# Splitting the first group's load 1 + 15 rows instead of 4 + 12 in a row-sum kernel

## The chip, the cores and the metric

The kernel runs on one core of one Trainium2 chip. The metric is the time of one execution on the device in microseconds (us). The profiled span, which begins with the first instruction, is some 1.8 us shorter than the timed value of the same execution.

## The reference

```python
def setup_inputs():
    batch, seq, dim = 32, 512, 1024
    return {"x": np.random.randn(batch, seq, dim).astype(np.float32)}

def reference(x):
    return np.sum(x, axis=-1).astype(np.float32)
```

That is 16,384 rows of 1,024 numbers, 67.1 MB to be read, and 64 KB to be written. Each number is added once.

## The kernel before

The rows are cut into eight groups of 8.39 MB. In a group each of the 128 partitions gets 16 consecutive rows of 4 KB. The sync engine (SP) issues all loads, on one queue. VectorE sums the rows, and ScalarE (ACT) helps at the end.

```python
    BIG = 16
    x_g = x.flatten_outer_dims().rearrange("(g p j) d -> g p j d", p=P, j=BIG)
    last = J // BIG - 1          # 7
    FIRST = 4
    ...
        tc.tile_pool(name="in", bufs=3) as inpool,
    ...
        def rows(t, a, n, j, n_act, pairs=False):
            nv = n - n_act
            block = t[:, a * dim : (a + n) * dim].rearrange("p (n d) -> p n d", d=dim)
            load = nc.sync.dma_start(out=block, in_=rows_from(j, n))
            ...
                sums_of.append(vec(sums[:, j : j + nv], block[:, :nv, :]))
    ...
        for g in range(last):
            t = inpool.tile([P, BIG * dim + 4], fp32)
            if g == 0:
                rows(t, 0, FIRST, 0, 0)
                first = sums_of[-1]
                rows(t, FIRST, BIG - FIRST, FIRST, 0)
                continue
            load = rows(t, 0, BIG, g * BIG, BIG // 2 if g == last - 1 else 0)
            if g == 1:
                hold(load, first, "no descriptors of later loads while the first ones start")
    # ... group 7 in smaller and smaller loads (8, 5, 2 rows, then one row in two pieces), and the stores
```

Group 0 arrives in two loads, so VectorE can begin before all of it is there. The load of group 1 is held until the first reduce has ended. There are three input buffers, so the load of group 3 waits until VectorE has finished with group 0.

## Time and profile before

| | before |
|---|---|
| time, median | 161.9 us (161.78 to 162.58) |
| span | 160.2 us |
| queue of the loads, share of 16 DMA engines' time | 97.7% |
| VectorE busy | 75% |
| period of a middle group | 19.35 us for 8.39 MB = 433.5 GB/s |

First look for the resource that is never idle. These are lines of the profile page of the kernel before: VectorE (DVE) busy time, its share and its number of instructions; then the DMA queues with packets, megabytes and share.

```profile
span 160.2 us, 125 instructions
DVE 120.1 (75%) x22; ACT 17.3 (11%) x31; POOL 0.2 (0%) x4
q1 hardware_dynamic: 2016, 67.12, 97.7%
```

The queue q1 carries the loads and is full for nearly the whole span. VectorE has a quarter of the time to spare. The timeline of VectorE shows where it spends that quarter. Its columns are start, duration, the operation with its shapes, and in brackets the idle time before it and what ended it.

```profile
7.16 4.42 DVE L130 TENSOR_REDUCE sums<-t 128x4 f32<-128x4096 f32 x1 [7.16 <-DMA t<-in_x_dram]
21.68 12.95 DVE L130 TENSOR_REDUCE sums<-t 128x12 f32<-128x12288 f32 x1 [10.10 <-DMA t<-in_x_dram]
41.05 17.22 DVE L130 TENSOR_REDUCE sums<-t 128x16 f32<-128x16384 f32 x1 [6.42 <-DMA t<-in_x_dram]
60.40 17.22 DVE L130 TENSOR_REDUCE sums<-t 128x16 f32<-128x16384 f32 x1 [2.13 <-DMA t<-in_x_dram]
...
137.82 8.69 DVE L130 TENSOR_REDUCE sums<-t 128x8 f32<-128x8192 f32 x1 [2.15 <-DMA t<-in_x_dram]
```

Every wait is for a load. VectorE always catches up (17.22 us of work for 19.35 us of data) and then waits 2.13 us.

The trace has a record of every DMA packet (start, duration, size). A packet here is one partition's contiguous piece of one load, and each of the 16 DMA engines carries 8 packets of each load. Usual durations are 611 ns for 16 KB, 1815 for 48 KB and 2418 for 64 KB. With these and the smaller ones, an engine's packets of the whole input take 155.07 us. The first data packet starts 1.0 us after the first issue, and the last one ends at 157.44 us. So the stream loses only 1.4 us in all (157.44 - 1.00 - 155.07).

### The profile page before, as it was taken

What the parts mean: (1) busy time and instruction counts of PE and PEld (TensorE: products, weight loads), DVE (VectorE), ACT (ScalarE), POOL (GpSimd) and SP (SyncE); (2) the same over time, 40 slices, a digit from 0 to 9 for tenths busy, and PEclk for the clock granted to TensorE, in tenths of its full rate; (3) what the DMA queues carried; (4) which work ended last, traced back from release to release, by engine and by line L of the source; (5) the groups of instructions that cost most, each with busy time, mean ns of one, the idle gap of its engine ahead of it and who ended that gap; (6) DMA issues with size and microseconds to landing.
All of it is one profiled execution on the core that took longest, in us unless ns stands there. A gap on an engine that the chain in (4) does not pass through costs nothing.

```text
span 160.2 us, 125 instructions
## 1 busy us (share of the span) xinstructions
DVE 120.1 (75%) x22; ACT 17.3 (11%) x31; POOL 0.2 (0%) x4
## 2 busy tenths in 40 slices
DVE  0280059960799959999499994999949998597943
ACT  3000000000000000000000000000000000596952
POOL 0000000000000000000000000000000000000000
DMA  7999996996996996996996997998969969999994
GB/s 262 458 466 515 393 523 262 523 523 262 523 523 262 523 523 262 523 523 262 523 491 294 523 458 327 523 409 376 523 262 523 523 262 523 393 393 425 409 379 112
DMA packets 2928, 67.18 MB, mean 419 GB/s; under 512 B 1264, under 2 KB 1392, under 8 KB 1520
## 3 DMA queue, kind: packets, MB, share of 16 engines
q1 hardware_dynamic: 2016, 67.12, 97.7%
q10 hardware_dynamic: 912, 0.06, 0.4%
HBM read 67.11 MB, written 0.07 MB: 419 GB/s over the span
## 4 chain that ended last, share of the span: by engine, by line
DMA 73%; DVE 25%; SPq 1%; issue 0%; DVEq 0%
DMA t<-in_x_dram 73%; DVE sums L130 24%; SPq L169 1%; SPq L210 0%; DVE t L144 0%; DVEq L241 0%
## 5 line engine op out<-in xcount | busy, mean ns | idle before, releaser
L130 DVE TENSOR_REDUCE sums<-t 128x16 f32<-128x16384 f32 (+3 forms) x9 | 116.6, 12953 | 35.5 <-DMA t<-in_x_dram 35.5
L157 ACT ACTIVATE unread<-t 128x1024 f32<-128x1024 f32 x15 | 15.2, 1010 | 139.6 <-DMA t<-in_x_dram 139.6
L144 DVE CUSTOM_DVE_ANT_0 t<-t 128x512 f32<-128x512 f32 (+2 forms) x6 | 3.5, 603 | 2.7 <-DMA t<-in_x_dram 2.6
L157 ACT ACTIVATION_READ_ACCUMULATOR unread<-t 128x1 f32 x15 | 2.8, 186 | 0.0
L157 ACT ACT_TABLE_LOAD x1 | 1.3, 1283 | 0.8 <-PEq L230 0.8
L144 DVE DVE_READ_ACCUMULATOR2_ANT sums<- 128x1 f32 x5 | 0.4, 84 | 0.0
L230 POOL MEMSET const-bfloat16-1.0<- 128x1 bf16 x1 | 0.1, 102 | 0.0
L230 POOL MEMSET const-uint8-127<- 128x1 uint8 x1 | 0.1, 102 | 0.0
L230 POOL MEMSET const-float32-0.0<- 128x1 f32 x1 | 0.1, 99 | 0.2 <-issue 0.2
L230 POOL MEMSET const-float32-1.0<- 128x1 f32 x1 | 0.1, 99 | 0.0
L144 DVE DVE_READ_ACCUMULATOR2_ANT t<- 128x1 f32 x1 | 0.1, 82 | 0.0
L208 DVE MEMSET t<- 128x1 f32 x1 | 0.1, 59 | 0.0
## 6 DMA issues: line engine op xcount, KB each, us to landing
t<-in_x_dram SPq DMA_DIRECT2D x1, 6144.0 KB, 20.9
t<-in_x_dram SPq DMA_DIRECT2D x1, 4096.0 KB, 31.3
t<-in_x_dram SPq DMA_DIRECT2D x1, 2560.0 KB, 37.3
t<-in_x_dram SPq DMA_DIRECT2D x1, 2048.0 KB, 7.1
t<-in_x_dram SPq DMA_DIRECT2D x1, 1024.0 KB, 39.3
t<-in_x_dram SPq DMA_DIRECT2D x1, 280.0 KB, 39.5
t<-in_x_dram SPq DMA_DIRECT2D x1, 232.0 KB, 39.6
t<-in_x_dram SPq DMA_DIRECT2D x6, 40.8
```

Source lines behind the costliest of these rows:

```text
L130: return nc.vector.tensor_reduce(out=dst, in_=src, axis=mybir.AxisListType.X, op=mybir.AluOpType.add)
L144: return nc.vector.tensor_tensor_reduce(out=src[:, :n], in0=src[:, :n], in1=src[:, n:], scale=1.0, scalar=0.0, op0=mybir.AluOpType.add, op ...
L157: nc.scalar.activation(out=unread[:, :n], in_=src, func=mybir.ActivationFunctionType.Copy, accum_out=dst,)
L169: load = nc.sync.dma_start(out=block, in_=rows_from(j, n))
L208: nc.vector.memset(whole[:, width + 1 :], 0.0)
L230: nc = _bacc.Bacc("TRN2", target_bir_lowering=False, num_devices=1)
```

## The change

The intent is to let VectorE start earlier: the first load is a quarter of the size, and the second has the other 15 rows. By the hold, the load of group 1 is also issued earlier.

```diff
     last = J // BIG - 1
-    FIRST = 4
+    FIRST = 1
     pieces = (560, 464)
```

## The prediction

> What bounds the kernel now. The DMA stream. The page shows 67.18 MB in a 160.2 us span; one queue's packets fill 97.7% of 16 engines' time. In the timeline VectorE starts group 1 at 41.05, group 2 at 60.40, up to 137.82 us: 19.35 to 19.37 us per 8.39 MB group, 433.5 GB/s. That agrees with the fabric ceiling of 435 GB/s in the Trainium skill, "DMA: Bandwidth & Descriptors", section "Where 436 GB/s comes from". VectorE is busy 75% and waits about 2.1 us for each load. The packet records show data on all 16 engines from 1.0 to 1.8 us after the first issue to 157.4 us, with gaps of at most 0.17 us: only the stream's start, its packets, and the tail after 157.4 us set the time.
>
> What the change moves. The first group is still two loads of 128 packets each, 8 per engine, same bytes, same order. Packet sizes go from 16 KB + 48 KB to 4 KB + 60 KB. Packet times before: 611 ns for 16 KB, 1815 for 48 KB, 2418 for 64 KB, 309 for 8 KB, so about 37.7 ns per KB plus some 8 ns per packet. Estimates: 4 KB 159 ns, 60 KB 2268. The pair sums to 2.43 us both ways, so stream time is unchanged.
>
> Start. Each engine's first packet took 0.74 to 1.47 us instead of 0.61, about 0.5 us of cold start. I expect it once per engine again, not per packet. The first load should land at about 7.1 minus 3.6 us (1.57 MB at 433.5 GB/s): 3.5 us, estimate. The second load is issued at 0.78 us in both; data followed the first issue by 1.0 us, so its packets should be ready by about 1.9 us, before the first load's packets run out near 2.8 us. No gap.
>
> VectorE. The reduce of four rows took 4.42 us and of twelve 12.95; of one row I estimate 1.22, of fifteen 16.15 (1.067 us per row plus 0.15). That load lands at 21.7 us as before, so its reduce ends at about 37.8 instead of 34.6 us. Group 1's data comes at 41.05: slack shrinks from 6.4 to about 3.2 us. Group 3's load waits for that buffer and is issued at 37.9 instead of 34.7 us; groups 1 and 2 keep the queue full until 60 us, so 22 us of cover remain. So nothing reaches the critical path.
>
> Hold. Group 1's load waits for the first reduce's end: now near 4.8 us, not 11.6. At 11.6 to 12.5 us before, with two issues, no 48 KB packet took over 1.825 us: no visible cost. And 4.8 us is after the cold packets, which ended by 2.9 us.
>
> Predicted: 161.9 us, range 161.4 to 162.6. Chances: faster by over 2% 0.01, within 2% 0.96, slower by over 2% 0.03.
>
> What would show it: same group starts at 41.05, 60.40 ... (within 0.3 us); idle before the fifteen-row reduce about 17 us instead of 10.1; last data packet near 157.4 us; the reduce of fifteen at 16.1 us.
>
> What would make it wrong: small first packets that each pay the cold start, or a second load whose descriptors come late, opening a gap at 2 to 4 us (up to about 1 us); the earlier issue of groups 1 and 2 slowing the stream at 5 us; 60 KB packets slower per byte than 48 and 64 KB ones.

## The result and the profile after

The changed kernel took 162.24 us (median of 6 runs, 162.05 to 162.25), the kernel before 161.97 us (6 runs, 161.78 to 162.58). The ratio is 1.0006, with a 95% interval of 0.9987 to 1.0025. Ratios here are the mean time of one kernel's runs over that of the other's of the same rounds, so not quite the ratio of the medians quoted.

The same lines of the page, of the changed kernel:

```profile
span 160.5 us, 125 instructions
DVE 120.1 (75%) x22; ACT 17.3 (11%) x31; POOL 0.2 (0%) x4
q1 hardware_dynamic: 2016, 67.12, 97.5%
```

And the timeline of its VectorE:

```profile
3.87 1.22 DVE L130 TENSOR_REDUCE sums<-t 128x1 f32<-128x1024 f32 x1 [3.87 <-DMA t<-in_x_dram]
22.28 16.15 DVE L130 TENSOR_REDUCE sums<-t 128x15 f32<-128x15360 f32 x1 [17.19 <-DMA t<-in_x_dram]
41.63 17.22 DVE L130 TENSOR_REDUCE sums<-t 128x16 f32<-128x16384 f32 x1 [3.20 <-DMA t<-in_x_dram]
...
138.38 8.69 DVE L130 TENSOR_REDUCE sums<-t 128x8 f32<-128x8192 f32 x1 [2.12 <-DMA t<-in_x_dram]
```

VectorE does start 3.29 us earlier (3.87 instead of 7.16 us). It then waits 17.19 us for the second load instead of 10.10. The larger second reduce leaves 3.20 us of slack before group 1 instead of 6.42.

One thing was not predicted. Group 1 starts at 41.63 instead of 41.05 us, 0.58 us later, although the bytes and the number of packets are the same. The packet records place it. In the table below, "excess" is the sum of the packets' durations over their usual ones, divided by 16, so that it is time per DMA engine.

| packet records | before | changed |
|---|---|---|
| first load: usual packet; excess | 611 ns; 0.58 us | 159 ns; 0.60 us |
| second load: usual packet; excess | 1815 ns; 0.00 us | 2267 ns; 0.33 us |
| second load: the 16 engines end | 20.97 to 21.27 us | 21.32 to 21.92 us |
| excess of the 32 KB and 20 KB packets (group 7) | 0.44 us | 0.02 us |
| last data packet ends | 157.44 us | 157.53 us |

The cold start costs the same 0.6 us with small packets as with large ones. But the second load's packets lost 0.33 us per engine, all of it in packets that started between 3 and 13 us, and the engines ended further apart. The reduce waits for the last engine, hence the 0.58 us. By the end of the stream only 0.1 us of it was left, since in this pair of profiles the kernel before lost 0.42 us more in its last group. (The balance is not negative because each engine of the changed kernel also spent 0.2 us more without a packet, 0.32 instead of 0.12.)

### The profile page after: what moved, and what is told of

Read it like the earlier page. It is cut to its first block, busy times and chain, and to the rows that moved or that the text cites. A ratio compares the mean times of both kernels' runs of the same rounds, so it can differ in the third digit from the quotient of the medians.

```text
span 160.5 us, 125 instructions
## 1 busy us (share of the span) xinstructions
DVE 120.1 (75%) x22; ACT 17.3 (11%) x31; POOL 0.2 (0%) x4
## 4 chain that ended last, share of the span: by engine, by line
DMA 75%; DVE 22%; SPq 1%; issue 0%; DVEq 0%
DMA t<-in_x_dram 75%; DVE sums L130 22%; SPq L169 1%; SPq L210 0%; DVE t L144 0%; DVEq L241 0%
## 5 line engine op out<-in xcount | busy, mean ns | idle before, releaser
L130 DVE TENSOR_REDUCE sums<-t 128x16 f32<-128x16384 f32 (+4 forms) x9 | 116.6, 12953 | 35.9 <-DMA t<-in_x_dram 35.9
## 6 DMA issues: line engine op xcount, KB each, us to landing
t<-in_x_dram SPq DMA_DIRECT2D x1, 7680.0 KB, 21.5
```

What stands on the lines that cost most here:

```text
L130: return nc.vector.tensor_reduce(out=dst, in_=src, axis=mybir.AxisListType.X, op=mybir.AluOpType.add)
```

## The experiments

Three questions are open. Is the prediction's reason right, that there is an unused reserve of time between VectorE and the stream (main theory), or do a gain and a loss merely cancel? How large is the reserve, and what would use it up? And where do the 0.33 us come from: from issuing groups 1 and 2 at 5.1 us, while the second load is young (theory I), or from the packets themselves (theory P)? Twelve runs were made: two repeats and ten other kernels. All gave correct results. A stream or an engine is said to run dry when it has no packet left to carry.

### The changed kernel and the kernel before, once more

No edit.

> The changed kernel once more, as a control. Main theory (the input stream sets the time, and the change leaves its bytes and its number of packets alone): 162.0 to 162.4 us, ratio to before within 0.4%. In the first profile of the changed kernel the 128 packets of 60 KB took together 0.32 us per DMA engine more than 2.267 us each, all before 12.5 us, and group 1 started at 41.63 instead of 41.05 us. If that belongs to the change it is here again (0.2 to 0.4 us per engine, group 1 at 41.4 to 41.8); if it was chance it is not (under 0.1, group 1 at about 41.1).

Measured: 162.13 us (ratio 1.0006, interval 0.9986 to 1.0025). The excess of the 60 KB packets is 0.34 us, and group 1 starts at 41.58 us. It came again, so it belongs to the change.

> The kernel before once more, as a control. 161.7 to 162.2 us. If the missing excess in the second load is its property, its 48 KB packets again take under 0.05 us per engine over 1.815 us, and group 1 starts at 41.0 to 41.4. In its first profile the late loads (32 KB and 20 KB packets) took 0.44 us per engine over their usual time, which the changed kernel's did not: if that is a property of it, it is here again (over 0.3); if chance, under 0.15.

Measured: 161.83 us (ratio to itself 1.0001). The second load's excess is again 0.00 us, and group 1 starts at 41.23 us. The excess in the last group is 0.22 us, between the two numbers expected. So the loss there is not settled as a property of the kernel before; it varies. Last data packet: 157.24 us, against 157.49 in the repeated changed kernel. It was run at another time.

### The hold at its old time, with one row first

```diff
                 rows(t, 0, FIRST, 0, 0)
+                for _ in range(5):
+                    sums_of.append(vec(sums[:, 0:1], t[:, :dim].rearrange("p (n d) -> p n d", d=dim)))
                 first = sums_of[-1]
```

> One-row first load, but its reduce is done six times, so that the loads of groups 1 and 2 are issued at about 11.2 us as before, not at 5.1. Theory I (the slow 60 KB packets come from issuing two large loads while the second load starts): their excess falls under 0.05 us per engine and group 1 starts at about 41.1. Theory P (they come from the small first packets or the 60 KB form itself): the excess stays 0.2 to 0.4 us per engine and group 1 starts at about 41.6. Both: the time stays within 0.4% of before, 161.8 to 162.4.

Measured: 162.26 us (ratio 1.0014, 0.9994 to 1.0034). Groups 1 and 2 were issued at 11.13 and 11.51 us. The excess is 0.33 us all the same, and group 1 starts at 41.59. VectorE's lines of this run:

```profile
3.62 7.49 DVE L130 TENSOR_REDUCE sums<-t 128x1 f32<-128x1024 f32 x6 [3.62 <-DMA t<-in_x_dram]
22.24 16.15 DVE L130 TENSOR_REDUCE sums<-t 128x15 f32<-128x15360 f32 x1 [11.13 <-DMA t<-in_x_dram]
41.59 17.22 DVE L130 TENSOR_REDUCE sums<-t 128x16 f32<-128x16384 f32 x1 [3.20 <-DMA t<-in_x_dram]
```

Theory I falls: with the issues put back to their old time, group 1 is as late as in the changed kernel.

### No hold at all, with one row and with four

```diff
-            if g == 1:
-                hold(load, first, "no descriptors of later loads while the first ones start")
```

> One-row first load and no hold: groups 1 and 2 are issued right after the second load, at 1.2 to 2 us. Main theory: 162.0 to 162.6, the packets are the same. Theory I adds an excess of 0.3 us or more per engine in the first two loads. Rival (the hold matters, and the small time difference hides a gain by one cause and a loss by another): over 163 us.

Measured: 162.14 us (ratio 1.0006), groups 1 and 2 issued at 1.15 and 1.63 us, an excess of 0.24 us, group 1 at 41.46 us. The 60 KB packets are slow as before, no slower.

> The kernel before without its hold: groups 1 and 2 issued at 1.2 to 2 us instead of 11.6. Main theory: 161.8 to 162.5. Theory I: the 16 KB and 48 KB packets now take 0.2 to 0.5 us per engine more than their usual 0.611 and 1.815 us beyond the cold start (before: 0.58 us of cold start and nothing on the 48 KB packets), and group 1 starts at 41.3 to 41.7. Theory P: as before, group 1 at about 41.05.

Measured: 161.89 us (ratio 0.9998, 0.9972 to 1.0023). The 48 KB packets have an excess of 0.00 us. The cold start is 0.56 us, and the last data packet ends at 157.23 us. So the hold buys nothing measurable here, and the early issue disturbed nothing. In this run group 1 started at 41.32 us because the engines ended their second load 0.64 us apart, with no excess at all; that spread came from the cold start, where one engine's first packet began at 1.90 us.

### The split moved the other way

```diff
-    FIRST = 1
+    FIRST = 12
```

> The same split moved the other way: 12 rows first, 4 second, the hold kept. Here the issue of group 1 does reach the critical path by the account of the stream: the first load lands at about 16.7 us, its reduce ends at 29.6, group 1 is issued then and its data starts 1.0 us later, while the first two loads end at 21.3. A gap of about 9.3 us in the DMA stream at 21 to 31 us, all later groups 9.3 us later, time about 171.3 us (170.3 to 172.3). If the place of the split and of the hold never matters, 162.

Measured: 172.42 us (ratio 1.0653, 1.0637 to 1.0669), just outside the expected range. Here the hold waits for a reduce that ends at 29.9 us, long after the two loads have. The view of three stretches of this run, with columns busy time of VectorE, ScalarE and GpSimd, clock, DMA share and GB/s:

```profile
16.00:21.00 5.00, 4.06 (x1) 0.00 (x0) 0.00 (x0) 1.00 0.98 419
21.00:31.00 10.00, 10.00 (x2) 0.00 (x0) 0.00 (x0) 1.00 0.12 39
31.00:36.00 5.00, 3.22 (x1) 0.00 (x0) 0.00 (x0) 1.00 0.86 341
```

The stream is dry for 9.7 us per engine (0.12 of a DMA share in the middle line). The expected gap of 9.3 us left out the restart: data came from the first engine 0.95 us after the issue and from the last 1.88 us after it, and each engine's first packet then took 0.64 us more than usual. That is a second cold start, as long as the one at entry.

### More vector work in group 0

```diff
                 rows(t, FIRST, BIG - FIRST, FIRST, 0)
+                for _ in range(N):      # N = 1: done twice; N = 2: three times
+                    sums_of.append(vec(sums[:, FIRST:BIG], t[:, FIRST * dim : BIG * dim].rearrange("p (n d) -> p n d", d=dim)))
```

> The changed kernel with the 15-row reduce done twice: 16.15 us more of vector work, five times what the change added there. Account of the cover: it ends at 54.6 us, before group 3's buffer is needed at about 60.9, and VectorE regains 2.13 us in each later group, just in time for the last loads. Time unchanged, 162.0 to 162.6. If vector work in the first group is on the critical path: 178.

Measured: 162.16 us (ratio 1.0021, 1.0006 to 1.0036). The 16.15 us of added work moved the end by about as much as the unchanged one-row kernel's own difference. The view of the waits gives the total in us, their number and the longest. In the changed kernel the reduces of line 130 waited for their data as follows:

```profile
DVE sums L130 <- DMA t<-in_x_dram: 35.9, 9, 17.2
```

In this run they waited less; the second line has the waits for the last small loads:

```profile
DVE sums L130 <- DMA t<-in_x_dram: 21.0, 2, 17.5
DVE t L144 <- DMA t<-in_x_dram: 1.8, 2, 1.1
```

Apart from the two waits of group 0, only 1.8 us are left, before the last small loads. So nearly all of the later slack of VectorE was used, and none of the stream: group 3's load was issued at 54.55 us, still 5.3 us before the first engine would have run dry.

> The 15-row reduce three times: 32.3 us more of vector work. It ends at 70.7 us, group 3's load is issued then instead of at 38.5, after the stream has run dry at 60.9: a gap of about 10.8 us in the stream, and VectorE still behind at the end. Worked out step by step: 177 us (175.5 to 178.5). If all of the added work counted: 194; if none: 162.

Measured: 176.49 us (ratio 1.0905, 1.0886 to 1.0923). The next step of the same size costs 14.3 us. Group 3's load was issued at 71.05 us, while the stream ran dry at 60.0 to 60.8. The view of three stretches shows it:

```profile
50.00:60.00 10.00, 9.97 (x2) 0.00 (x0) 0.00 (x0) 1.00 0.97 419
60.00:73.00 13.00, 13.00 (x2) 0.00 (x0) 0.00 (x0) 1.00 0.22 76
73.00:83.00 10.00, 10.00 (x1) 0.00 (x0) 0.00 (x0) 1.00 0.98 426
```

In the second run the last data packet ends 12.9 us later than in the changed kernel, and the span grows by 14.4: the other 1.5 us are VectorE's, which still lags behind when the last data arrive. So vector work in group 0 meets two limits: an issue that comes too late for the stream, and VectorE's catching up before the last loads, which the first run had nearly reached. That work was free at 16.15 us and not at 32.3; where in between it begins to cost was not measured.

### Two buffers instead of three

```diff
-        tc.tile_pool(name="in", bufs=3) as inpool,
+        tc.tile_pool(name="in", bufs=2) as inpool,
```

> The changed kernel with two buffers instead of three: group 3's load is issued when group 1's reduce ends, at 58.9 us, about 2.0 us before the stream would run dry, and data follows an issue by 1.0 us. Account of the cover: 162.2 to 163.5 us, no gap or a few tenths per group. Rival (the third buffer is what hides the change): five gaps of 1 us or more, over 167 us.

Measured: 168.83 us (ratio 1.0433, 1.0388 to 1.0478). The account of the cover missed here, and the time is in the rival's range. VectorE's timeline in this run:

```profile
61.28 17.22 DVE L130 TENSOR_REDUCE sums<-t 128x16 f32<-128x16384 f32 x1 [2.14 <-DMA t<-in_x_dram]
82.44 17.22 DVE L130 TENSOR_REDUCE sums<-t 128x16 f32<-128x16384 f32 x1 [3.94 <-DMA t<-in_x_dram]
102.34 17.22 DVE L130 TENSOR_REDUCE sums<-t 128x16 f32<-128x16384 f32 x1 [2.68 <-DMA t<-in_x_dram]
123.97 17.22 DVE L130 TENSOR_REDUCE sums<-t 128x16 f32<-128x16384 f32 x1 [4.41 <-DMA t<-in_x_dram]
```

The period of 19.35 us has become 19.9 to 21.6 us. Group 3 was issued at 59.17 us. The earliest engine ran dry at 59.96, only 0.80 us later, and not at 60.82, when the last one did. In this run the records put together 4.2 us of added idle time per engine (4.55 instead of 0.33) and 2.8 us of added excess (3.96 instead of 1.13), which makes up the 6.9 us of longer span. The excess is mostly cold first packets again, 0.22 to 0.58 us on average in each of the five loads after group 2. The engines drift apart as well: they end group 3 over 1.9 us, and group 5 over 2.8 us, where group 2 ended over 0.9.

The next kernel is the one before, with two buffers, to see whether the narrower spread of four rows first saves it.

> The kernel before, with two buffers. With one row first, two buffers gave 168.8 us: the earliest engine ran dry at 59.96 us, 0.80 us after group 3's issue, and data needs 1.1 us from issue to an idle engine. With four rows first the engines end within 0.3 us of one another instead of 0.9, so the cover is 1.34 us (58.30 to 59.64). Theory (the spread between engines decides): no gap, 161.9 to 163. Rival (two buffers are too few in any case): about 167 to 170, as with one row.

Measured: 167.52 us (ratio 1.0348, 1.0332 to 1.0364). The theory falls. In this run the engines ended group 2 at 59.55 to 60.12 us, 1.06 to 1.62 us after the issue, and the first packets of group 3 still took 0.56 us too long and began as late as 60.77 us. So the 1.0 to 1.1 us after which the first data are seen are not lead enough. What is enough stays open. Group 2 of the other two-buffer run, issued at 38.75 and needed by its engines at 40.64 to 41.51, started with no gap and no cold packet, at leads of 1.88 to 2.75 us. But group 4 of the same run, issued at 78.53 and needed at 80.19 to 82.07, had leads of 1.67 to 3.54 us; nearly every engine went on without a gap, and still every first packet took too long, by 0.22 us on average. Whether the lead does that, or the engines' drift in the group before, was not separated. Leads over 5.3 us (group 3 with the 15-row reduce done twice, group 2 here) were clean.

Two buffers are thus too few with either split: the third buffer is needed, but not because of the change. The two kernels with two buffers ran in different submissions, so their difference of 1.3 us is not put down to the split.

### The offset of the second load

Row 15 is loaded first, then rows 0 to 14, so the 60 KB packets begin where the 64 KB of a partition begin.

```diff
-                rows(t, 0, FIRST, 0, 0)
+                rows(t, BIG - FIRST, FIRST, BIG - FIRST, 0)
                 first = sums_of[-1]
-                rows(t, FIRST, BIG - FIRST, FIRST, 0)
+                rows(t, 0, BIG - FIRST, 0, 0)
```

> The one-row first load takes row 15 of each partition instead of row 0, so the 60 KB packets start at multiples of 64 KB in the input, as those of the kernel before never did for its second load. Theory of offset (reads that begin 4 KB into each 64 KB are slow): the excess of the 60 KB packets falls under 0.1 us per engine, group 1 at about 41.2. Theory of order (small first packets leave the 16 engines at moments that disturb one another until the third to fifth packet): the excess stays at 0.2 to 0.4 us. Time within 0.4% of before in both.

Measured: 162.19 us (ratio 1.0023, 1.0010 to 1.0035), with an excess of 0.54 us, over the range of both theories, and group 1 at 41.70 us. The offset is not the cause either. Taken in the order of their starts, sixteen at a time (one for each engine), this load's packets lose on average 0.03 and 0.06 us in the first two lots, 0.20 and 0.19 in the next two, 0.05 in the fifth, and nothing after it; the changed kernel shows the same course. What is left is that a load of one row comes first, or the size of 60 KB in this place: no run had one without the other. (Where 48 KB or 64 KB packets came first of all, in the runs with 12 rows first and with one load, none of them was slow after each engine's first.) How packets become slow some 5 us later was not found.

### One load, no split, no hold

```diff
-                rows(t, 0, FIRST, 0, 0)
-                first = sums_of[-1]
-                rows(t, FIRST, BIG - FIRST, FIRST, 0)
+                rows(t, 0, BIG, 0, 0)
                 continue
             ...
-            if g == 1:
-                hold(load, first, "no descriptors of later loads while the first ones start")
```

> No split and no hold: the first group is one load of 64 KB packets, with one reduce of 16 rows. Main theory (the first load's only effect is an early start of VectorE, which the stream does not need): 161.7 to 162.3 us, group 1 at 41.0 to 41.4; 8 packets per engine less, 8 ns each, cannot be seen. If the split earns its place: 163 or more.

Measured: 162.35 us (ratio 1.0027, 1.0014 to 1.0039), barely over the expected 162.3, group 1 at 41.41 us. Without any early start VectorE waits only 2.15 us before group 1 and is in time all the same:

```profile
22.04 17.22 DVE L130 TENSOR_REDUCE sums<-t 128x16 f32<-128x16384 f32 x1 [22.04 <-DMA t<-in_x_dram]
41.41 17.22 DVE L130 TENSOR_REDUCE sums<-t 128x16 f32<-128x16384 f32 x1 [2.15 <-DMA t<-in_x_dram]
```

So the split with its hold is worth at most a few tenths of a microsecond here, with four rows or with one. That answers the first question too: with the early start gone altogether there is no large loss, so no large gain was there for a loss to cancel. No version beat the kernel before. The kernel without the hold equals it with less code.

## Why the prediction was right

Predicted were 161.9 us (161.4 to 162.6), and 162.24 were measured.

- **The stream bounds the kernel.** Right. Group 0's vector work could grow by 16.15 us at no visible cost, while one gap of 9.7 us in the stream cost 10.7 us.
- **Same bytes, same number of packets, same stream time.** Nearly right. The durations were hit to a nanosecond (159 and 2267 ns against 159 and 2268). The sum was not: the second load's packets took 0.24 to 0.54 us per engine more than usual in all eight profiles of kernels with a one-row load in front. The prediction named two possible reasons for such a loss, an earlier issue and slower 60 KB packets. The first is refuted (late hold, no hold). The second isn't it in general: the 60 KB packets that start after 13 us (15 us in one run) have their usual time.
- **A cold start once per engine, not per packet.** Right: 0.60 us against 0.58. The first load was expected at 3.5 us; VectorE started at 3.87 here and at 3.60 in the repeat.
- **No gap before the second load.** Right. Its packets start at 2.89 us, directly behind the first load's.
- **VectorE.** Right. One row took 1.22 us and fifteen 16.15, both as estimated. The slope, 1.067 us for 1,024 numbers, is 0.96 numbers per nanosecond and partition, which agrees with the clock of 0.96 GHz that the Trainium skill gives in "VectorE: DVE Perf Modes", section "Specifications". The slack of about 3.2 us was measured at 3.20.
- **Group 3's issue.** Predicted at 37.9, seen at 38.46 us, some 21.5 us before the stream needed it. The runs with more vector work show it used up somewhere between 16.15 and 32.3 us of added work.
- **Group starts within 0.3 us.** Wrong: group 1 came 0.58 us later. The loss shrank to 0.10 us at the last data packet in this pair of profiles, and to 0.25 us in the repeated pair. That so little was left in the first pair is luck: the kernel before happened to lose 0.44 us in its last group, against 0.22 us in its repeat.

The medians of the one-row kernels whose VectorE work was not multiplied lie at 162.13 to 162.24 us, those of the kernel before at 161.76 to 161.97. Within one submission the medians differ by 0.3 to 0.4 us, but the means, from which the ratios are made, by only 0.1 us in three of the four (ratio 1.0006), because single runs of the kernel before took up to 162.58 us. A cost of 0.1 to 0.4 us is thus likely, but it was resolved from noise only in the variant that loads the last row first (ratio 1.0023) and in the one with the 15-row reduce done twice (1.0021).

## What to carry to other kernels

If a stream of transfers is full from its first packet to its last, an earlier start of the consumer is given back as a longer wait; ask first whether the stream would end sooner. The reserve of the stream is the time by which each issue precedes the moment at which the earliest DMA engine, not the last, runs dry; the consumer has a second one, the waits in which it can catch up before the last loads. Within both much can be moved at no cost; beyond the first, the gap counts in full here, plus a cold restart. An issue needs more lead than the 1.0 us after which the first data are seen: here leads of 0.8 to 1.7 us were too short, those over 5.3 us were enough, and in between the runs disagree.

## What the Trainium skill lacked or had wrong

- "DMA: Bandwidth & Descriptors", section "Where 436 GB/s comes from", states that for transfers between HBM and SBUF the HBM side of about 358 GB/s binds. These loads from HBM ran at 433.5 GB/s on one core (8.39 MB in 19.35 us), close to the fabric ceiling. The sentence lacks its condition, which the page's section "Measured (HBM→SBUF, 128 partitions, SWDGE, issued from GpSimd)" has: its 425 GB/s for 16 MB are a single-core number, and about 358 GB/s are what each core gets when both of a pair stream.
- The same page, section "Latency and other measured facts", gives about 600 ns to the first byte of a transfer issued from the sync engine. Here the first packet record started 0.95 to 1.13 us after an issue to idle engines, and the last engine's first packet 1.4 to 2.0 us after it where all were idle. (How the start of a record relates to the first byte, no run here shows.)
- No page that was consulted has the cost of letting the stream run dry: the first packets of the engines then took on average 0.57 and 0.64 us longer than usual in the two runs where all of them had run dry (the first load at entry lost 0.47 to 0.69 us per engine). A lead of 1.06 to 1.62 us did not avoid it, leads of 1.88 to 2.75 us did in one load, and leads of 1.67 to 3.54 us in another left 0.22 us of it.
- None of them has what was seen in the load behind a one-row load: its 60 KB packets lost 0.24 to 0.54 us per engine, mostly among the first four of each engine's eight, in all eight profiles that had it. The cause is open.
